# Delta rule of a hybrid decoder layer: the inverse applied to the residual inside the chain, fill products tied to the chain's links, and zero-block buffers made once

## The chip, the cores and the metric

The kernel runs on one core of one Trainium2 chip. The metric is the device time of one execution in microseconds (us); lower is better. The core has a matrix engine (TensorE; PE in the profile, with its weight loads as PEld), a vector engine (DVE), a scalar engine (ScalarE; ACT), a general engine (GpSimd; POOL) and a queue for loads and stores (SyncE; SP). Each engine works through its own list of instructions and waits for the others by semaphores.

## What is computed

One decoder layer: an RMS norm, one input projection, then two mixers side by side (a gated delta rule over 4 heads of 128, and dilated attention over 8 heads of 64), gates, and one output projection with the residual. The sequence has 2048 tokens. The part that matters here is the delta rule, in chunks of 64 tokens:

```python
l_mat = a_mat + jnp.eye(CHUNK)                       # a_mat strictly lower
u = triangular_solve(l_mat, vc * bc[..., None])
w = triangular_solve(l_mat, kb * jnp.exp(gc)[..., None])
...
def step(state, inp):
    a_i, qd_i, kt_i, u_i, w_i, gl_i = inp
    v_new = u_i - jnp.einsum('bhck,bhkv->bhcv', w_i, state)
    o_i = jnp.einsum('bhck,bhkv->bhcv', qd_i, state) + jnp.einsum('bhij,bhjv->bhiv', a_i, v_new)
    state = state * gl_i[..., None, None] + jnp.einsum('bhck,bhcv->bhkv', kt_i, v_new)
    return state, o_i
```

Since `u` and `w` are the same inverse applied to two right sides, `v_new` is also that inverse applied to the difference `beta v - exp(g) beta k state`. The state goes from chunk to chunk, 32 steps in a row for each head.

## The kernel before

The kernel projects the sequence (`conv_proj`, `gate_proj`: `pj` products of 128x512), prepares the inverses of the triangular matrices (`stage1a`, `inverse`), runs the delta rule, and then attention and the output projection. Projections and output use pairs of high and low parts, three products for one.

The delta rule handles heads in two pairs; a pair's two heads lie side by side in the 128 partitions, 64 tokens each. Four chunks make a group.

- `stage2` (L614, 16 calls: 8 groups by 2 pairs) prepares a group of one pair. It loads `kT`, `qT`, `vT`, the rows `Qr`, the mask `E`, the inverse's blocks `TT` and `D0`; completes the inverse with 32x32 products (L650, L657); forms `at` (L665, L674), the squares of q (L662, in a buffer `tmp`) and their sums (L668); turns k and v (L688); scales them to `Kc` (L691), `Ks` (L694) and `kV` (L698). Then `pw = Kc TT` (L701), copied into `WQ` (L704), and `pu = TT kV` (L707), copied to `U` (L709), each four products. The other half of `WQ` is q times `Qr` (L634, GpSimd). Buffers with blocks of zeros (`at_`, `Ks`) are set to zero by GpSimd in every call (L670, L671, L681, L682); `TT` has two buffers that are zeroed once.
- `chain` (L720, 64 calls) is one chunk of one pair: two `C` products of the state with `WQ` (L727), two vector additions to `VN` (L731), two `SU` products (L733), two vector operations to the new state `S` (L737), the product with `at` (L741), its copy (L742), two additions to the output `o4` (L745) and its squares (L747). `SU` is one tile for both pairs; `C` has two buffers.
- `dn_out` (L749) scales a group's output (`zs`, L762) and stores it.
- `proj_fill` (L908) is the attention's input projection: 2304 `pj` products of 128x256 in 12 sets of 192, with the splitting of its weights (`wh` on ScalarE, `wl` on the vector engine, 1024 columns) and the work behind a finished tile (`t`, `ss`, `qs`, products `pm`). These products are the fills: they have the lowest priority, and the first 960 (`HOLD * 192`, L963) may go before the chain's end.

The order on each engine is set when the program is built: a scheduler takes, at each point, the ready instruction with the lowest priority number, where `chain` starts at 1000000, `dn_out` too, `stage2` at 1200000, the second gate projection at 1900000 and the fills at 2400000. `add_manual_dep(..., NOSYNC)` ties an instruction behind another in the order of the same engine, without a semaphore. A buffer that is written again waits for its readers.

I call both pairs' work on one chunk a link.

Of the kernel before, what the change touches and what calls it, by code (L numbers as in the profile page):

```python
# [16 lines left out]
P = 128  # L17
# [20 lines left out]
HOLD = 5  # L38
PATT0 = 2400000
# [45 lines left out]
def hybrid(tc, xT, x, norm_w, w_in, conv_w, a_log, dt_bias, dn_norm_w, q_norm_w, k_norm_w,  # L85
# [521 lines left out]
    TTz = [dn.tile([P, 4, P], F32, name=f"TTz{i}") for i in range(2)]  # L607
    for t in TTz:
        nc.gpsimd.memset(t[:CH, :, CH:], 0.0)
        nc.gpsimd.memset(t[CH:, :, :CH], 0.0)  # L610
    turn2 = [0]
    SU = psD.tile([P, 4, P], F32, name="SU", bufs=1)

    def stage2(pair, c0, dma2=dma):  # L614
# [18 lines left out]
        for s_ in range(2):  # L633
            nc.gpsimd.tensor_tensor(WQ[:, :, s_, (1 - s_) * CH:(2 - s_) * CH], Qr[:, :, s_], qT[:, :, 1 - s_],  # L634
                                    op=ALU.mult)
# [25 lines left out]
        q2 = dn.tile([P, 4, P], F32, name="tmp", bufs=2)  # L661
# [7 lines left out]
        at_ = dn.tile([P, 4, P], F32, name="at_", bufs=3)  # L669
        nc.gpsimd.memset(at_[:CH, :, :CH], 0.0)  # L670
        nc.gpsimd.memset(at_[CH:, :, CH:], 0.0)  # L671
# [8 lines left out]
        Ks = dn.tile([P, 4, 2, P], F32, name="Ks", bufs=3)  # L680
        nc.gpsimd.memset(Ks[:CH, :, 1], 0.0)  # L681
        nc.gpsimd.memset(Ks[CH:, :, 0], 0.0)  # L682
        Kc = dn.tile([P, 4, P], F32, name="tmp", bufs=2)
        kV = dn.tile([P, 4, P], F32, name="tmp", bufs=2)
        for w, src in enumerate((kT, vT)):
            tp = psD.tile([P, 4, P], F32, name="A", bufs=2)
            for u in range(4):
                nc.tensor.transpose(tp[:, u], src[:, u].rearrange("p s i -> p (s i)"), ident)  # L688
            if w == 0:
                for u in range(4):  # L690
                    nc.scalar.mul(Kc[:, u], tp[:, u], negc_u[:, u0 + u:u0 + u + 1])  # L691
                for s_ in range(2):
                    a = slice(s_ * CH, (s_ + 1) * CH)
                    nc.vector.tensor_tensor(Ks[a, :, s_], tp[a], sk[a, 0, :, None].to_broadcast([CH, 4, P]),  # L694
                                            op=ALU.mult)
# [3 lines left out]
        pw = psD.tile([P, 4, P], F32, name="A", bufs=2)  # L699
        for u in range(4):  # L700
            nc.tensor.matmul(pw[:, u], Kc[:, u], TT[:, u], start=True, stop=True)  # L701
        for s_ in range(2):
            a = slice(s_ * CH, (s_ + 1) * CH)
            nc.vector.tensor_copy(WQ[:, :, s_, a], pw[:, :, a])  # L704
        pu = psD.tile([P, 4, P], F32, name="A", bufs=2)
        for u in range(4):
            nc.tensor.matmul(pu[:, u], TT[:, u], kV[:, u], start=True, stop=True)  # L707
# [3 lines left out]
        return dict(WQ=WQ, at=at_, Ks=Ks, U=U, o4=o4, D0=d0)  # L711
# [3 lines left out]
    for pair in range(2):  # L715
        s0 = dn.tile([P, 2, P], F32, name=f"S{pair}", bufs=2)
        nc.vector.memset(s0, 0.0)
        Sst.append(s0)

    def chain(pair, c, g):  # L720
# [4 lines left out]
        pc, po, su = pcs[:, 0:2], pcs[:, 2], SU[:, 2 * pair:2 * pair + 2]  # L725
        for s_ in range(2):
            nc.tensor.matmul(pc[:, s_], g["WQ"][:, u, s_], S0[:, s_], start=True, stop=True)  # L727
        VN = dn.tile([P, P], F32, name="VN", bufs=4)
        for s_ in range(2):
            a = slice(s_ * CH, (s_ + 1) * CH)  # L730
            nc.vector.tensor_tensor(VN[a], pc[a, s_], g["U"][a, u], op=ALU.add)  # L731
        for s_ in range(2):
            nc.tensor.matmul(su[:, s_], g["Ks"][:, u, s_], VN, start=True, stop=True)  # L733
        S1 = dn.tile([P, 2, P], F32, name=f"S{pair}", bufs=2)
        for s_ in range(2):
            h = 2 * pair + s_
            m = nc.vector.scalar_tensor_tensor(S1[:, s_], S0[:, s_], egl[c % 2][:, h * NT + c // 2:h * NT + c // 2 + 1],  # L737
                                           su[:, s_], op0=ALU.mult, op1=ALU.add)
        Sst[pair] = S1
        mark[c] = m  # L740
        mark["pe"] = nc.tensor.matmul(po, g["at"][:, u], VN, start=True, stop=True)  # L741
        nc.scalar.copy(g["o4"][:, u], po)  # L742
        for s_ in range(2):
            b = slice((1 - s_) * CH, (2 - s_) * CH)
            nc.vector.tensor_tensor(g["o4"][b, u], pc[b, s_], g["o4"][b, u], op=ALU.add)  # L745
# [162 lines left out]
    def proj_fill():  # L908
# [4 lines left out]
        n = 0  # L913
        for s_ in range(12):
# [3 lines left out]
            for o8 in range(8):  # L918
# [30 lines left out]
                for kt in range(KT):  # L949
# [5 lines left out]
                    for x_, w_ in ((xh, 0), (xh, 1), (xl, 0)):  # L955
                        while posts and posts[0][0] <= n:
                            posts.pop(0)[1]()
                        if s_ < 11 and o8 == 7 and kt == 2 and w_ == 0 and x_ is xh:
# [3 lines left out]
                                             stop=kt == KT - 1 and x_ is xl)  # L962
                        if n == HOLD * 192:  # L963
# [600 lines left out]
```

## Time and profile before

| what | us |
|---|---|
| median of 3 runs (lowest, highest) | 1385.46 (1384.54, 1389.88) |
| the profiled execution | 1385.32 |
| its span | 1383.5 |
| TensorE busy in 480 to 780 us by `pj` products of 128x256 (three groups of rows) | 96.1, 95.0, 94.8 |
| TensorE busy, 750 to 800 us, of 50 | 45.54 |
| TensorE busy, 800 to 900 us, of 100 | 96.62 |

How to read it: a row of a group names the line, the engine, the operation and the tiles (out <- in), then a count, busy time and mean; behind it stands the idle time of the engine just ahead of those instructions, and what ended it. A row of the timeline has its start, its length, and in brackets the idle time ahead of it. A product of float32 has two records, and `x4` of L733 is two products. Matmuls overlap, so the distance between the starts, not the length, is what one costs TensorE; the chain of waits shows that distance. Clock is the granted share of TensorE's full clock.

### The profile page before, as it was taken

How to read it: one execution, taken by the hardware profiler on the slowest of the kernel's cores; microseconds unless marked ns; L12 is line 12 of the kernel's file. 1: busy time of each engine (PE TensorE's matmuls, PEld its weight loads, DVE VectorE, ACT ScalarE, POOL GpSimd, SP SyncE). 2: the span in 40 equal slices, each digit the busy share in tenths (PEclk: the TensorE clock that was granted, in tenths of full speed). 3: DMA queues.
4: the chain of work that ended last, by engine and by line, in shares of the span. 5: the costliest groups of instructions: out<-in, count | busy, mean ns of one | idle time of the engine just before them, and what ended most of it. 6: DMA issues, size and time to landing. Idle time of an engine off the chain costs nothing.

```text
span 1383.5 us, 28812 instructions
## 1 busy us (share of the span) xinstructions
PE 1360.6 (98%) x10262; PEld 1215.8 (88%) x10262; DVE 857.3 (62%) x2724; ACT 675.8 (49%) x1930; POOL 484.7 (35%) x572
## 2 busy tenths in 40 slices
PE   8999999999999999999999999999999999999998
PEld 7998787778888789999999889999998888888877
DVE  7534668899652358787787565635454746555565
ACT  5644525573322234444444476566666655555520
POOL 3000000000761204442342423574857384655500
PEclk9999999999999999999999999999999999999999
DMA  6654526756647846657553455264647786655764
GB/s 191 185 105 90 110 57 146 162 128 116 110 84 143 205 108 155 156 147 195 132 149 78 108 138 134 78 185 97 177 116 240 200 253 162 198 163 175 207 196 144
DMA packets 301324, 205.01 MB, mean 148 GB/s; under 512 B 149324, under 2 KB 271068, under 8 KB 300669
## 3 DMA queue, kind: packets, MB, share of 16 engines
q1 hardware_dynamic: 230652, 171.09, 49.3%
q10 hardware_dynamic: 70528, 32.09, 8.5%
q8 instruction: 81, 1.33, 0.4%
q14 instruction: 63, 0.51, 0.1%
HBM read 142.61 MB, written 60.50 MB: 147 GB/s over the span
## 4 chain that ended last, share of the span: by engine, by line
PE 85%; DVE 6%; DMA 4%; ACT 3%; issue 2%; ACTq 0%; SPq 0%; POOL 0%; DVEq 0%
PE pj L99 18%; PE po L99 10%; PE sc L99 8%; PE pj L208 7%; PE pj L207 7%; PE pj L206 7%; PE pz L99 6%; PE pv L99 5%; PE pt L99 4%; PE SU L733 2%; PE C L727 2%; PE pm L99 1%; PE A L665 1%; PE A L688 1%; PE A L701 1%
## 5 line engine op out<-in xcount | busy, mean ns | idle before, releaser
L99 PE MATMUL pj<-wh,xh 128*128 128x256 f32 (+1 forms) x776 | 226.9, 292 | 1.3 <-DVE ml L99 1.3
L99 ACT ACTIVATE pr<-pr,ml 128x192 f32<-128x192 f32 (+2 forms) x384 | 156.8, 409 | 146.1 <-DVE ml L99 132.3
L99 PE MATMUL pj<-wh,xl 128*128 128x256 f32 (+1 forms) x776 | 224.6, 289 | 0.0
L99 PE MATMUL pj<-wl,xh 128*128 128x256 f32 (+1 forms) x776 | 224.3, 289 | 0.0
L208 PE MATMUL pj<-xh,wl 128*128 128x512 f32 x512 | 203.5, 397 | 0.7 <-DVE wl L192 0.7
L206 PE MATMUL pj<-xh,wh 128*128 128x512 f32 x512 | 202.6, 396 | 0.0
L207 PE MATMUL pj<-xl,wh 128*128 128x512 f32 x512 | 202.6, 396 | 0.0
L99 PE MATMUL po<-xh,mh 128*128 128x512 f32 x424 | 147.9, 412 | 1.0 <-ACT mh L99 0.7
L99 PEld LDWEIGHTS pj<-wh,xh 128*128 128x128 f32 x776 | 146.4, 189 | 2.5 <-issue 2.2
L99 PEld LDWEIGHTS pj<-wh,xl 128*128 128x128 f32 x776 | 146.5, 189 | 0.5 <-issue 0.3
L99 PEld LDWEIGHTS pj<-wl,xh 128*128 128x128 f32 x776 | 146.6, 189 | 0.1
L99 DVE CUSTOM_DVE_ANT_0 pr<-sc,bias 128x192 f32<-128x192 f32 (+2 forms) x384 | 100.0, 307 | 68.6 <-PE sc L99 67.7
L478 DVE SCALAR_TENSOR_TENSOR cy<-cu,cw,cy 128x512 f32<-128x512 f32 x144 | 111.6, 775 | 19.3 <-ACT cy L476 17.1
L208 PEld LDWEIGHTS pj<-xh,wl 128*128 128x128 f32 x512 | 96.2, 188 | 23.3 <-DVE wl L192 1.1
L207 PEld LDWEIGHTS pj<-xl,wh 128*128 128x128 f32 x512 | 96.2, 188 | 22.2
L206 PEld LDWEIGHTS pj<-xh,wh 128*128 128x128 f32 x512 | 96.3, 188 | 21.7
L99 POOL COPY qz<-q 64x512 f32<-64x512 f32 x96 | 95.0, 989 | 51.7 <-PE sc L99 38.8
L99 DVE COPY pT<-pt 64x128 f32<-64x128 f32 (+2 forms) x220 | 69.4, 323 | 64.7 <-PE pt L99 61.3
L543 POOL MEMSET inv<- 128x1024 f32 x1 | 1.0, 954 | 259.5 <-DVE cu L474 259.5
L99 POOL TENSOR_TENSOR Fb<-Fb,op 128x256 f32<-128x256 f32 x84 | 71.5, 865 | 57.6 <-DMA Fb<-F 29.7
L99 PEld LDWEIGHTS po<-xh,mh 128*128 128x128 f32 x424 | 77.9, 189 | 14.2 <-DVE mh L99 1.2
L99 PE MATMUL po<-xl,mh 128*128 128x512 f32 x212 | 86.5, 408 | 0.0
(371 smaller groups left out, 3068.5 us busy)
## 6 DMA issues: line engine op xcount, KB each, us to landing
wraw<-in_w_in SPq DMA_DIRECT2D x44, 512.0 KB, 7.1
cv<-cy ACTq DMA_DIRECT2D x48, 256.0 KB, 2.6
Fb<-F SPq DMA_DIRECT2D x64, 192.0 KB, 5.2
xr<-in_xT SPq DMA_DIRECT2D x32, 256.0 KB, 4.0
kT<-cv SPq DMA_DIRECT2D x32, 256.0 KB, 3.3
qk<-qs ACTq DMA_DIRECT2D x64, 128.0 KB, 4.2
res<-in_x SPq DMA_DIRECT2D x13, 512.0 KB, 4.9
V<-v_d SPq DMA_DIRECT2D x20, 256.0 KB, 4.9
```

The lines of the kernel that those rows point to most:

```text
L99: i = f(*args, **kw)
L206: nc.tensor.matmul(ps, wh[:, k, c * P:(c + 1) * P], xh[tb][:, kt, :], start=kt == 0, stop=False)
L207: nc.tensor.matmul(ps, wh[:, k, c * P:(c + 1) * P], xl[tb][:, kt, :], start=False, stop=False)
L208: nc.tensor.matmul(ps, wl[:, k, c * P:(c + 1) * P], xh[tb][:, kt, :], start=False, stop=kt == KT - 1)
L478: nc.vector.scalar_tensor_tensor(y, u[:, i:i + 512], cw[:, ct, i:i + 1], y, op0=ALU.mult, op1=ALU.add)
L543: eng.memset(Tt, 0.0)
L665: nc.tensor.matmul(pq[:, u], kT[:, u].rearrange("p s i -> p (s i)"), qT[:, u].rearrange("p s i -> p (s i)"), start=True, stop=True)
L688: nc.tensor.transpose(tp[:, u], src[:, u].rearrange("p s i -> p (s i)"), ident)
L701: nc.tensor.matmul(pw[:, u], Kc[:, u], TT[:, u], start=True, stop=True)
L727: nc.tensor.matmul(pc[:, s_], g["WQ"][:, u, s_], S0[:, s_], start=True, stop=True)
L733: nc.tensor.matmul(su[:, s_], g["Ks"][:, u, s_], VN, start=True, stop=True)
```

## The change

1. **The inverse in the chain.** `stage2` no longer makes `Kc`, `pw`, `pu` and `U`. The half of `WQ` that held `pw` now holds k itself, copied by GpSimd. In `chain` the two `C` products give k (and q) times the state; the vector engine forms the residual `R = kV - exp(g) C`; one more product (`TT`, L727 of the new program) applies the inverse; ScalarE copies the result to `VN`. Chunk 0 has no state, so it skips the `C` products and the additions to the output; chunk 31 skips the `SU` products and the new state.
2. **Fills held to the links.** For the links of chunks 1 to 30, a dictionary `gates` ties fills 0, 15, 23 (then 32 more for each link) behind the last `WQ`, `TT` and `SU` product of that chunk: 15, 8 and 9 fills a link, 960 in all.
3. **Zero blocks in lists.** `TT` has four buffers, `at` and `Ks` three; their zeros are written once, at the start. The squares of q go to the buffer of `Qr`; `kV` has a buffer of its own.
4. **Pair 1's preparation** is written behind the group's four links, no longer behind the first.

```diff
+LINK0 = 1
+FILL = (15, 8, 9)
...
+    TTs = zeroed("TT", 4, [P, 4, P], True)
+    ATs = zeroed("at", 3, [P, 4, P], False)
+    KSs = zeroed("Ks", 3, [P, 4, 2, P], "half")
...
+            nc.gpsimd.tensor_copy(WQ[:, :, s_, s_ * CH:(s_ + 1) * CH], kT[:, :, s_])
...
-        TT = TTz[n2 % 2]
+        TT = TTs[n2 % 4]
...
-        q2 = dn.tile([P, 4, P], F32, name="tmp", bufs=2)
+        q2 = Qr.rearrange("p u s i -> p u (s i)")
...
-                for u in range(4):
-                    nc.scalar.mul(Kc[:, u], tp[:, u], negc_u[:, u0 + u:u0 + u + 1])
...
-        for u in range(4):
-            nc.tensor.matmul(pw[:, u], Kc[:, u], TT[:, u], start=True, stop=True)
...
-            nc.vector.tensor_copy(WQ[:, :, s_, a], pw[:, :, a])
...
-            nc.tensor.matmul(pu[:, u], TT[:, u], kV[:, u], start=True, stop=True)
-        U = dn.tile([P, 4, P], F32, name="U", bufs=3)
-        nc.scalar.copy(U, pu)
...
+        R = g["kV"][:, u]
+        if c:
+            for s_ in range(2):
+                mark[c, 0] = nc.tensor.matmul(pc[:, s_], g["WQ"][:, u, s_], S0[:, s_], start=True, stop=True)
+            R = dn.tile([P, P], F32, name="R", bufs=2)
+            for s_ in range(2):
+                a = slice(s_ * CH, (s_ + 1) * CH)
+                nc.vector.scalar_tensor_tensor(R[a], pc[a, s_], negc_u[a, col:col + 1], g["kV"][a, u],
+                                               op0=ALU.mult, op1=ALU.add)
+        mark[c, 1] = nc.tensor.matmul(pn, g["TT"][:, u], R, start=True, stop=True)
+        VN = dn.tile([P, P], F32, name="VN", bufs=3)
+        nc.scalar.copy(VN, pn)
+        S1 = None
+        if c < 31:
+            for s_ in range(2):
+                mark[c, 2] = nc.tensor.matmul(su[:, s_], g["Ks"][:, u, s_], VN, start=True, stop=True)
...
-            if u == 0:
-                for p_ in range(2):
-                    if c0 + 4 < 32:
-                        G[p_] = at_prio("prep", stage2, p_, c0 + 4)
+            if u == 0 and c0 + 4 < 32:
+                G[0] = at_prio("prep", stage2, 0, c0 + 4)
+        if c0 + 4 < 32:
+            G[1] = at_prio("prep", stage2, 1, c0 + 4)
...
+        gates, k = {}, 0
+        for c in range(LINK0, 31):
+            for part in range(3):
+                gates[k] = (c, part)
+                k += FILL[part]
...
+                        if n in gates:
+                            tc.add_manual_dep(m.ins, mark[gates[n]].ins.name, NOSYNC, reason="no sooner than this link")
```

How this moves instructions, at three places. The numbers in the names tell buffers apart: `S_...` is a state, `at_...`, `Ks_...` and `TT_...` a pair's buffer of a group; `pj` rows are fills.

First, TensorE inside a link. Before, near the middle of the stage, this stands between the `SU` products of the two pairs; nine more fills follow the last row, and then the other pair's `SU`:

```order
L733 MATMUL SU<-VN,Ks 128x128 x2
L741 MATMUL C<-VN,at__5609 128x128
L657 MATMUL A<-TTz_4473,Xs 32x32 x6
L741 MATMUL C<-VN,at__5507 128x128
L657 MATMUL A<-TTz_4473,Xs 32x32 x2
L665 MATMUL A<-qT,kT 128x128 x4
L99 MATMUL pj<-wh,xl_139 128x256
```

In the change, the link of chunk 30 has this, and so have eight other links:

```order
L733 MATMUL SU<-VN,Ks_4496 128x128 x2
L744 MATMUL C<-VN,at_4487 128x128
L744 MATMUL C<-VN,at_4485 128x128
L733 MATMUL SU<-VN,Ks_4494 128x128 x2
L101 MATMUL pj<-wh,xh_140 128x256
L101 MATMUL pj<-wl,xh_140 128x256
```

The fills that stood between the pairs now stand behind the second `SU`.

Second, TensorE at the chain's end. Before, these rows are the last links, with the next fill four rows after the last one shown:

```order
L727 MATMUL C<-S_7294,WQ 128x128 x2
L733 MATMUL SU<-VN,Ks 128x128 x2
L741 MATMUL C<-VN,at__7074 128x128
L741 MATMUL C<-VN,at__6972 128x128
L733 MATMUL SU<-VN,Ks 128x128 x2
L727 MATMUL C<-S_7311,WQ 128x128 x2
L727 MATMUL C<-S_7328,WQ 128x128 x2
L733 MATMUL SU<-VN,Ks 128x128 x2
L741 MATMUL C<-VN,at__7074 128x128
L741 MATMUL C<-VN,at__6972 128x128
L733 MATMUL SU<-VN,Ks 128x128 x2
```

In the change, chunk 31 alone stands between fills:

```order
L101 MATMUL pj<-wh,xl_141 128x256
L721 MATMUL C<-S_7131,WQ 128x128 x2
L721 MATMUL C<-S_7151,WQ 128x128 x2
L727 MATMUL C<-R,TT_4475 128x128
L744 MATMUL C<-VN,at_4487 128x128
L727 MATMUL C<-R,TT_4476 128x128
L744 MATMUL C<-VN,at_4485 128x128
L101 MATMUL pj<-wh,xh_138 128x256
```

The fills that were used up earlier now last to the end of chunk 30.

Third, the vector engine where a group begins (one of the middle groups before, chunk 12 in the change). Before, one pair's outputs `zs` (L762) stand here, and the other pair's come a link later:

```order
L737 SCALAR_TENSOR_TENSOR S_5735<-S_5701,egl_120,SU 128x128 x2
L731 TENSOR_TENSOR VN<-C,U 64x128 x2
L759 SCALAR_TENSOR_TENSOR f<-ssqo,f 128x4
L675 COPY ssqq<-A 128x4
L694 TENSOR_TENSOR Ks<-A,sk 64x4x128 x2
L762 SCALAR_TENSOR_TENSOR zs<-o_5189,f,zs 128x128 x4
L731 TENSOR_TENSOR VN<-C,U 64x128 x2
L737 SCALAR_TENSOR_TENSOR S_5752<-S_5718,egl_120,SU 128x128 x2
L745 TENSOR_TENSOR o_5291<-C,o_5291 64x128 x2
```

In the change, behind the residual of pair 1 (the row ahead of the first one shown is a small one):

```order
L765 SCALAR_TENSOR_TENSOR zs<-o_5103,f,zs 128x128 x4
L684 TENSOR_TENSOR at_4487<-A,E_5726 64x4x64 x2
L761 TENSOR_SCALAR f<-ssqq 128x4
L765 SCALAR_TENSOR_TENSOR zs<-o_5301,f,zs 128x128 x4
L738 SCALAR_TENSOR_TENSOR S_5683<-S_5538,egl_119,SU 128x128 x2
L761 TENSOR_SCALAR f<-ssqq 128x4
L101 TENSOR_TENSOR wl<-wraw,wh 128x4x256
L748 TENSOR_TENSOR o_5446<-C,o_5446 64x128 x2
L748 TENSOR_TENSOR o_5644<-C,o_5644 64x128 x2
L699 TENSOR_TENSOR Ks_4496<-A,sk 64x4x128 x2
L685 COPY ssqq<-A 128x4
L738 SCALAR_TENSOR_TENSOR S_5703<-S_5558,egl_119,SU 128x128 x2
```

Both pairs' outputs, a weight split and the new `Ks` now stand between the residual of pair 1 and its new state.

More of the change, by code (lines that the diff above doesn't have):

```diff
@@ L679, in stage2 @@
         nc.gpsimd.tensor_tensor(sk[:, 1], sk[:, 1], phalf[:, :4], op=ALU.pow)
[L680 to L684, printed above, removed]
+        Ks = KSs[n2 % 3]
+        kV = dn.tile([P, 4, P], F32, name="kV", bufs=3)
         for w, src in enumerate((kT, vT)):
@@ L715, in hybrid @@
     for pair in range(2):
-        s0 = dn.tile([P, 2, P], F32, name=f"S{pair}", bufs=2)
-        nc.vector.memset(s0, 0.0)
-        Sst.append(s0)
+        Sst.append(None)
     def chain(pair, c, g):
@@ L724, in chain @@
         pcs = psD.tile([P, 4, P], F32, name="C", bufs=2)
[L725 to L738, printed above, removed]
+        pc, po, pn, su = pcs[:, 0:2], pcs[:, 2], pcs[:, 3], SU[:, 2 * pair:2 * pair + 2]
+        R = g["kV"][:, u]
[7 more added lines that the diff above has]
+                                               op0=ALU.mult, op1=ALU.add)
```

36 lines of the change are left out of this document (20 added, 16 removed).

## The prediction

> **What bounds the kernel now.** I read the page first, then busy time by stretch, then the chain of waits inside the stage that the change touches. That stage is the delta rule, whose `SU` products run from 484 to 777 us.
>
> ```profile
> L733 PE MATMUL SU<-VN,Ks x256: 270/275/377, 484.3 to 777.2; 128*128 128x128 f32 x128
> ```
> ```profile
> span 1383.5 us, 28812 instructions
> PE 1360.6 (98%) x10262; PEld 1215.8 (88%) x10262; DVE 857.3 (62%) x2724; ACT 675.8 (49%) x1930; POOL 484.7 (35%) x572
> ```
>
> The span is 1383.5 us; the profiled execution took 1385.3, so 1.8 lies around the span. The median of the runs shown is 1385.46, which is the same within 0.2 us, and I sum against 1385.3. The busy shares are an average, so the stage comes next (columns: stretch, length, busy us of PE, PEld, DVE, ACT, POOL, granted clock, DMA share, GB/s).
>
> ```profile
> 560.00:570.00 10.00, 10.00 (x101) 9.84 (x101) 8.87 (x28) 4.22 (x18) 6.32 (x12) 1.00 0.60 159
> 760.00:770.00 10.00, 8.72 (x70) 8.02 (x68) 6.90 (x19) 3.77 (x10) 2.81 (x4) 1.00 0.52 109
> 770.00:780.00 10.00, 7.85 (x56) 6.77 (x56) 8.54 (x31) 3.31 (x13) 1.86 (x2) 1.00 0.39 37
> ```
>
> TensorE is full in the middle of the stage and has holes only at its end. The vector engine stands close behind it, 8.87 of 10 us where a group of four chunks begins. The chain of waits (500 to 760 us, then pieces of 560 to 580) says the same: nearly all of it is TensorE.
>
> ```profile
> by line: PE pj L99 42.9%; PE C L727 10.1%; PE SU L733 9.7%; PE A L665 5.5%; PE A L688 5.2%; PE C L741 5.2%; PE A L701 4.8%; PE A L707 4.8%; PE A L668 4.2%; PE pm L99 2.2%; PE A L657 2.2%; PE A L650 2.2%; PE pm L596 0.6%; DVE ss L99 0.3%; DV
> ```
> ```profile
> 560.43 0.37 PE A L657 x16
> ...
> 563.36 0.44 PE SU L733 x4
> ...
> 564.25 0.79 PE A L668 x8
> ...
> 568.43 0.44 PE A L688 x4
> ...
> 572.42 0.89 PE A L707 x8
> 573.31 1.07 PE pj L99 x9
> ...
> 576.60 1.09 PE A L665 x8
> ```
>
> From these I take TensorE's prices. One float32 product of 128x128 is two records: 0.89 / 4 = 0.2225 us. One fill product is 1.07 / 9 = 0.119 us. So an instruction less on TensorE is time less, as long as something is always ready for it. Whether it is, is the question here.
>
> **What the change removes from TensorE.** Each of the 16 preparations loses `pw` (L701) and `pu` (L707), 8 products: 128 in all. Each of the 64 steps of the chain (32 chunks, 2 pairs) gains one, the inverse on the residual: 64. Chunk 0 loses its four products with the zero state, chunk 31 its four updates of a state that nobody reads: 8. Net 128 - 64 + 8 = 72 products, 72 x 0.2225 = **-16.0 us**. The 960 fill products ahead of the chain's end stay 960.
>
> **The end of the stage.** Today the fills run out three chunks early, and the last links stand bare:
>
> ```profile
> 765.48 0.61 PE L733 MATMUL SU<-VN,Ks 128*128 128x128 f32 x4
> ...
> 767.04 0.60 DVE L737 SCALAR_TENSOR_TENSOR S<-S,egl,SU 128x128 f32<-128x128 f32 x2
> ...
> 767.53 0.68 PE L727 MATMUL C<-S,WQ 128*128 128x128 f32 x4 [0.88 <-DVE S L737]
> ...
> 773.79 0.61 DVE L737 SCALAR_TENSOR_TENSOR S<-S,egl,SU 128x128 f32<-128x128 f32 x2 [0.18 <-PE SU L733]
> ```
> ```profile
> 774.45 0.71 PE L733 MATMUL SU<-VN,Ks 128*128 128x128 f32 x4 [0.25 <-DVE S L737]
> ...
> 776.81 0.71 PE L733 MATMUL SU<-VN,Ks 128*128 128x128 f32 x4 [0.96 <-DVE VN L731]
> ...
> 777.50 0.36 PE L99 MATMUL pj<-wh,xh 128*128 128x256 f32 x1
> ```
>
> From 765.48 to 777.50 are 12.0 us; in them the order has 27 products (6.0 us) and one fill, so 5.9 us are lost. With the fills dealt out by link only chunk 31 is bare. It has two hops (residual, then the copy of `VN`), and one such hop costs 0.96 in the row above: 1.9 us. Gain **-4.0 us**.
>
> **What the change adds: waits inside each link.** Now a low-priority fill goes wherever TensorE would be idle. After the change 15, 8 and 9 fills are tied behind the `WQ`, `TT` and `SU` products of a link, so no fill can stand elsewhere. What the vector engine needs is shown by its rows:
>
> ```profile
> 559.63 0.69 DVE L99 TENSOR_TENSOR t<-pj,ss 128x512 f32<-128x512 f32 x1
> ...
> 561.48 0.86 DVE L674 TENSOR_TENSOR at__5242<-A,E 64x256 f32<-64x256 f32 x2
> ...
> 563.84 0.61 DVE L737 SCALAR_TENSOR_TENSOR S<-S,egl,SU 128x128 f32<-128x128 f32 x2 [0.30 <-PE SU L733]
> ...
> 564.98 1.14 DVE L762 SCALAR_TENSOR_TENSOR zs<-o,f,zs 128x128 f32<-128x128 f32 x4
> ...
> 566.75 1.39 DVE L694 TENSOR_TENSOR Ks<-A,sk 64x512 f32<-64x512 f32 x2
> 568.17 0.59 DVE L731 TENSOR_TENSOR VN<-C,U 64x128 f32<-64x128 f32 x2
> ```
> ```profile
> 765.90 1.23 DVE L99 TENSOR_TENSOR wl<-wraw,wh 128x1024 fp32r<-128x1024 f32 x1 [1.48 <-ACT wh L99]
> ```
> ```profile
> 774.43 1.21 DVE L745 TENSOR_TENSOR o<-C,o 64x128 f32<-64x128 f32 x4
> ```
>
> *Bare link.* Pair 1's `SU` waits for pair 0's state update, since both lie in one tile: today at 774.45, 0.05 after the update's end. The update starts 0.48 after `SU` is issued (563.36 to 563.84) and lasts 0.61, so `SU` of pair 1 goes 1.14 after that of pair 0. TensorE has 0.44 and the two `at` products, 0.89, to do meanwhile. Wait 0.25. Nine links have nothing else there: 2.3 us.
>
> *Weight split.* In five links the vector queue has `wl` between the two pairs' updates, in two of them `t` as well. Pair 1's update then starts at 0.48 + 0.61 + 1.23 + 1.21 = 3.53, its second half is there at 4.19, and the last `WQ` product ends 0.22 later, at 4.41. TensorE alone would be there at 1.14 + 0.44 + 1.07 + 0.89 = 3.54. Wait 0.87, with `t` 1.56: 3 x 0.87 + 2 x 1.56 = 5.7 us. Behind a waiting `WQ` the whole queue of TensorE stands, fills too.
>
> *Group starts.* Both pairs' output products `zs` now fall into one link; today they are a link apart. In the worst group (rows in the section on the change) pair 1's update comes after two `zs` (2.28), `at` 0.86, `S` 0.61, `wl` 1.23, `o` 1.21, `Ks` 1.39 and some 0.3 of small ones: 7.9 us behind its residual, and `WQ` 0.49 later (767.04 to 767.53), 8.4. TensorE needs `TT` 0.22, eight fills 0.95, `SU` 0.44, `at` 0.45, `kT` 0.44, L668 0.79, `SU` 0.44, nine fills 1.07, `WQ` 0.45, `vT` 0.44, 0.37: 6.1, after a lag of about 1 us (15 fills 1.8 and L665 1.09 against `t`, a copy and two residuals, about 2): 7.1. Wait 1.3. In the link before, `at`, `Ks` and `o` ahead of pair 1's update cost 0.9 in the same way: 2.2. In the best group `Ks` is behind both updates, and some 0.6 is left. Seven groups at 1.4: 9.8 us; between the ends I take the middle, as the orders of the other groups lie between these two.
>
> Sum of the waits 2.3 + 5.7 + 9.8 = **+17.8 us**. Its ends: 2.3, if only the bare links wait; about 33, if each of 30 links waits 0.25 + 0.87.
>
> **What costs nothing, and its cover.**
>
> ```profile
> L691 ACT ACTIVATE tmp<-A,negc_u 128x128 f32<-128x128 f32 x60 | 17.1, 368 | 16.3 <-PE A L688 16.1
> ...
> L742 ACT COPY o<-C 128x128 f32<-128x128 f32 x64 | 16.7, 265 | 61.1 <-PE C L741 60.8
> ```
>
> ScalarE loses the 64 scalings of L691 (17 us) and the 16 copies `U`, and gains 64 copies of `VN` like L742 (17 us); at 4.2 busy of 10 it has room. A copy stands in the chain, 0.27 behind `TT`, under eight fills (0.95). Without that cover: 0.3 to 0.6 a link, 9 to 18 us. The vector engine loses the 32 copies of L704. GpSimd loses 64 memsets and gains 16 more at the start and 32 copies like L634 below, 0.73 each; it is busy 6.3 of 10 at its fullest above. At the start they stand ahead of the first `WQ`, which waits for `Qr` anyway: 0, at worst 3 us.
>
> Pair 1's preparation is written behind the four links, and its loads with it. On SP one `Qr` stands behind `y_d` and `zs`, and it waits for the products of L668, since the squares lie in its buffer.
>
> ```profile
> L631 SPq DMA_DIRECT2D Qr<-rows_d x32: 359/495/2879, 447.2 to 716.6; - x32
> ...
> DMA to landing us min/median/max: 3.6/4.6/6.7
> ```
> ```profile
> L643 SPq DMA_DIRECT2D TTz<-A x28: 573/588/2583, 476.1 to 721.7; - x28
> ...
> DMA to landing us min/median/max: 2.2/4.2/9.0
> ```
> ```profile
> L634 POOL TENSOR_TENSOR WQ<-Qr,qT x32: 721/731/1160, 456.1 to 742.0; 128x256 f32<-128x256 f32 x32
> ```
> ```profile
> L762 DVE SCALAR_TENSOR_TENSOR zs<-o,f,zs x64: 335/346/819, 526.3 to 782.5; 128x128 f32<-128x128 f32 x64
> ```
>
> Two issues of 0.5, 4.6 to land, three GpSimd operations of 0.73 and a square of about 0.6 make 8.4 us; TensorE asks for the squares a link and a half later, 9 to 10. The inverse's buffer is free only after a group's last link and is read about 6 us later; 1.2 + 4.2 = 5.4. Both fit at the median: 0. At the longest landings they miss by 1 and 4 us, up to 5 a group.
>
> **Sum.** 1385.3 - 16.0 - 4.0 + 17.8 = 1383.1; I say **1383 us**. Outside the stage nothing is added, and the attention behind it begins as soon as the chain ends.
>
> **Rivals.** *The fills cover the hops as they do today.* For it: in 500 to 760 us hardly a wait of TensorE is left, with the same vector work. Against it: those fills were free to go anywhere. Waits of 2.3 alone give 1385.3 - 20.0 + 2.3 = 1368 us (1364 to 1374).
>
> *The vector engine and late loads set the link's pace: slower.* Its work in the first link of a group (the 7.9 above, four half residuals, `t` and a copy, about 10.4 us) is more than TensorE's (6.1, then `WQ`, 15 fills and the rest, about 9), and a late `TT` or `Qr` stops TensorE's queue at the same place. It decides from a mean wait of 0.7 us a link: then 20 is lost. At 30 us it gives 1395 (1390 to 1402).
> On this the Trainium skill has a rule (SBUF — State Buffer, section Who interferes with whom): a vector instruction with two inputs in SBUF contends with a GpSimd instruction that reads SBUF, not with one that only writes. The change puts reading copies in place of writing memsets. The longest `zs`, 819 ns against 346, may be such a meeting, and the longest L634, 1160 against 731, too. By the rule the 14 groups of `zs` of the stage would lose up to 0.47 each, 6.6 us, and the time would be 1388. It has a small chance of its own, as both rows' medians lie at their shortest.
>
> *It doesn't do what it says:* the scheduler leaves fills out of place, or the removed products cost less than 0.2225 because they hid in other waits. Then some 1387.
>
> **How the numbers follow.** Forecast (waits take back most, 1372 to 1393) 0.5; cover holds 0.22; vector engine and loads 0.20; the meeting of vector engine and GpSimd 0.03; the last 0.05. A change below 0.5% (6.9 us) can't be told from none here, so "faster" is under 1378.4 and "slower" over 1392.2. Faster: 0.22 and a third of the forecast's case, 0.38. Slower: 0.20 and the last bit of the forecast's case, 0.22. Same: the rest, 0.40. The range reaches from the middle of the first rival to the middle of the second, with the waits' ends: 1366 to 1397.
>
> **What would show it.** Right: L701 and L707 gone, `SU` to `SU` in bare links 1.1 us apart, TensorE waits named `WQ` after `S` at five `wl` links and at group starts, the bare end shorter by 4 us, the time between first and last `SU` shorter by some 1 to 4 us. Wrong: TensorE busy throughout with no such waits (first rival), or waits at L668 and L650 for loads and 20 or more us of waits for the vector engine (second).

## The result and the profile after

| | before | after |
|---|---|---|
| median, us (lowest to highest) | 1387.05 (1384.54 to 1389.88), 4 runs | 1403.44 (1398.62 to 1408.89), 4 runs |
| ratio, with its 95% interval | | 1.0119 (1.01 to 1.0139) |
| the profiled execution, us | 1385.3 | 1408.89 |

The change makes the kernel 16 us slower; 1383 was forecast, 1366 to 1397 the range. The profiled execution of after is the slowest of its four, 5.4 us over the median. From the page and from the row of `SU`:

```profile
span 1407.0 us, 28403 instructions
PE 1363.5 (97%) x10118; PEld 1210.1 (86%) x10118; DVE 845.9 (60%) x2676; ACT 666.4 (47%) x1914; POOL 475.1 (34%) x556
```
```profile
L733 PE MATMUL SU<-VN,Ks x248: 270/275/583, 481.0 to 790.8; 128*128 128x128 f32 x124
```

TensorE has 144 records less, which are the 72 products, and is drawn busy 3 us longer. The stage's place is seen from the first fill behind the chain:

```profile
796.47 0.36 PE L101 MATMUL pj<-wh,xh 128*128 128x256 f32 x1
```

Before, that row stood at 777.50: the chain ends 19.0 us later. From there to the end of the span are 610.5 us, against 606.0 before. So 23.5 = 19.0 in the stage + 4.5 behind it.

**The work itself.** What TensorE's own work comes to can be estimated from starts: every record gets the mean distance to the next start that records of its shape have in before from 500 to 740 us (0.131 us for a fill, 0.108 for half a float32 product of 128x128). From 440 us to the chain's end this adds up to 331.9 us in before and 317.0 in after, 14.9 less. Priced by pairs of neighbouring shapes instead, it is 13.5 less. So the forecast's -16.0 came nearly whole, and the time was lost again elsewhere.

**Holes in the stage.** What TensorE waited for, 481 to 797 us (total, times, longest):

```profile
PE SU L733 <- DVE S L738: 4.3, 12, 1.1
PE C L721 <- DVE o L748: 4.0, 7, 0.9
PE SU L733 <- ACT VN L729: 2.9, 2, 2.5
PE A L695 <- issue: 2.4, 2, 1.2
PE A L662 <- PE C L721: 1.2, 2, 0.6
...
PE C L721 <- DVE S L738: 0.6, 3, 0.2
```

The whole list comes to 18.0 us in 35 holes. Before, from 484 to 778 us, it is some 3.3 in 6, all at the bare end:

```profile
PE SU L733 <- DVE VN L731: 1.6, 2, 1.0
PE C L727 <- DVE S L737: 1.1, 2, 0.9
PE C L741 <- DVE VN L731: 0.4, 1, 0.4
PE SU L733 <- DVE S L737: 0.3, 1, 0.3
```

And the list understates. In a bare link (one with nothing else for TensorE to do), on the timeline of after (start, length),

```profile
677.34 0.61 PE L733 MATMUL SU<-VN,Ks 128*128 128x128 f32 x4
677.78 0.61 PE L744 MATMUL C<-VN,at 128*128 128x128 f32 x4
678.65 0.71 PE L733 MATMUL SU<-VN,Ks 128*128 128x128 f32 x4 [0.25 <-DVE S L738]
```

four records cost 0.44 (677.34 to 677.78), so TensorE was free from 678.22, and the next product went at 678.65: 0.43 lost, 0.25 listed, because the last product's record is drawn 0.18 beyond the point at which the next could start. If the 29 further holes are like this one, that is some 5 us on top of 14.7, an estimate.

**The clock.** The longest hole on the timeline, with what ScalarE, GpSimd and the vector engine did, and busy time in the stretches after it (the granted clock is third from the end):

```profile
654.78 1.22 PE L733 MATMUL SU<-VN,Ks 128*128 128x128 f32 x4 [2.51 <-ACT VN L729]
```
```profile
653.95 0.63 ACT L674 ACTIVATE Qr<-qT 128x512 f32<-128x512 f32 x1 [3.36 <-POOL WQ L645]
654.48 0.41 ACT L729 COPY VN<-C 128x128 f32<-128x128 f32 x2
```
```profile
652.13 1.78 POOL L645 TENSOR_TENSOR WQ<-Qr,qT 128x256 f32<-128x256 f32 x1 [1.08 <-DMA Qr<-rows_d]
```
```profile
652.12 1.21 DVE L101 TENSOR_TENSOR wl<-wraw,wh 128x1024 fp32r<-128x1024 f32 x1
```
```profile
650.00:655.00 5.00, 2.49 (x21) 2.29 (x21) 4.85 (x15) 1.53 (x4) 3.48 (x3) 0.96 0.93 286
655.00:660.00 5.00, 5.00 (x37) 4.71 (x38) 3.16 (x9) 1.87 (x8) 0.00 (x0) 0.50 0.40 114
660.00:665.00 5.00, 5.00 (x37) 4.65 (x37) 1.47 (x5) 0.30 (x2) 0.00 (x0) 0.52 0.44 133
```

Read it backwards. `SU` waits for the copy of `VN`; that copy stands on ScalarE behind the squares of q, which are written into `Qr` and so wait for GpSimd to have read it, and GpSimd waits for the load of `Qr`; its product then takes 1.78 us (0.73 is usual) beside the vector engine's `wl`. The hole is 2.5 us, and behind it TensorE runs at half clock for 10 us: 37 records in each 5 us, and 58 in the 5 us that follow, so 4.9 us more are lost. In these stretches TensorE reads as fully busy. Two other places of the stage (455 to 460 at 0.66, 535 to 545 at 0.85 and 0.81) lose 3.4 in the same way. The Trainium skill (TensorE: Matmul & The Clock Gate, Part 1: The HAM clock gate) has half clock come after an idle window of about 3.4 us; here a hole of 2.5 was enough.

The chain ends 19.0 us later with 14.9 us less work, so 34 us are to be found: 14.7 of listed holes, 5 of unlisted, 8.3 of clock. Some 6 are left in steps too short for any list; where they lie isn't shown. The experiments turn to these.

**Behind the stage.** The timeline of after, then that of before: the first splits of the attention on the vector engine, and ScalarE's table load ahead of the first exponential.

```profile
814.60 2.99 DVE L101 SCALAR_TENSOR_TENSOR xl<-big,nw,xh 128x512 fp32r<-128x512 f32 x2 [3.95 <-ACT xh L101]
817.51 2.92 DVE L101 TENSOR_TENSOR wl<-wraw,wh 128x1024 fp32r<-128x1024 f32 x1
...
809.67 1.28 ACT L101 ACT_TABLE_LOAD   x1 [4.78 <-DMA qk<-qs]
810.97 0.35 ACT L101 ACTIVATE pr<-pr,ml 128x64 f32<-128x64 f32 x1
...
821.80 2.89 PE L101 MATMUL sc<-K,qz 128*128 128x192 f32 x8 [3.84 <-DVE ml L101]
```
```profile
794.40 1.42 DVE L99 SCALAR_TENSOR_TENSOR xl<-big,nw,xh 128x512 fp32r<-128x512 f32 x2 [2.74 <-ACT xh L99]
795.96 1.92 DVE L99 TENSOR_TENSOR wl<-wraw,wh 128x1024 fp32r<-128x1024 f32 x1
...
786.85 1.28 ACT L99 ACT_TABLE_LOAD   x1 [0.94 <-ACT qs L99]
790.64 0.35 ACT L99 ACTIVATE pr<-pr,ml 128x64 f32<-128x64 f32 x1 [2.51 <-DVE ml L99]
```

Before, the load was done 2.5 us ahead of the exponential. After, it comes only behind the wait for `ml`: the row names a transfer, but the vector engine's first `ml` ended at 809.59, and the load starts at 809.67. Everything behind it on ScalarE is 1.3 us later, and the splits (0.75 for each `xl` and 1.22 for `wl` at their medians) then lie for most of their length beside two long copies of GpSimd (814.40 to 819.35) and take about twice as long. TensorE waits 3.84, and its clock falls to 0.68 for 5 us.

### The profile page after: what moved, and what is told of

Its sections match the earlier page's. It is cut to its first block, busy times and chain, and to the rows that moved or that the text cites. A ratio compares the mean times of both kernels' runs of the same rounds, so it can differ in the third digit from the quotient of the medians.

```text
span 1407.0 us, 28403 instructions
## 1 busy us (share of the span) xinstructions
PE 1363.5 (97%) x10118; PEld 1210.1 (86%) x10118; DVE 845.9 (60%) x2676; ACT 666.4 (47%) x1914; POOL 475.1 (34%) x556
## 4 chain that ended last, share of the span: by engine, by line
PE 78%; DVE 8%; DMA 7%; issue 2%; ACT 2%; SPq 1%; POOL 0%; ACTq 0%; DVEq 0%; POOLq 0%
PE pj L101 15%; PE po L101 10%; PE sc L101 7%; PE pj L210 7%; PE pj L209 7%; PE pj L208 7%; PE pz L101 6%; PE pv L101 5%; PE pt L101 4%; PE SU L733 2%; PE C L721 2%; DMA V<-v_d 1%; PE pm L101 1%; DMA Qr<-rows_d 1%; PE C L727 1%
## 5 line engine op out<-in xcount | busy, mean ns | idle before, releaser
L480 DVE SCALAR_TENSOR_TENSOR cy<-cu,cw,cy 128x512 f32<-128x512 f32 x144 | 111.5, 775 | 19.5 <-ACT cy L478 17.5
L210 PEld LDWEIGHTS pj<-xh,wl 128*128 128x128 f32 x512 | 96.3, 188 | 23.5 <-DVE wl L194 1.0
L101 PEld LDWEIGHTS po<-xh,mh 128*128 128x128 f32 x424 | 77.9, 189 | 14.2 <-DVE mh L101 1.2
```

The lines of the kernel that those rows point to most:

```text
L101: i = f(*args, **kw)
L210: nc.tensor.matmul(ps, wl[:, k, c * P:(c + 1) * P], xh[tb][:, kt, :], start=False, stop=kt == KT - 1)
L480: nc.vector.scalar_tensor_tensor(y, u[:, i:i + 512], cw[:, ct, i:i + 1], y, op0=ALU.mult, op1=ALU.add)
```

## The experiments

Cover is the other work that TensorE has while a link waits for another engine. Theories: **A**, the ties hold fills out of the holes; **B**, the squares' buffer puts a load in front of the `VN` copies; **C**, pair 1's preparation is too late; **D**, a link with two more hops needs more cover than there is, and the removed products were cover; **E**, a hop hides under free fills. Later **F** (the shared `SU` tile), **G** (the shares 15, 8, 9), **H** (the table load). Medians are compared with before on the same chip.

### Ties away, squares apart, preparation back, ties alone

```diff
-                        if n in gates:
-                            tc.add_manual_dep(m.ins, mark[gates[n]].ins.name, NOSYNC, reason="no sooner than this link")
```

> The kernel after, with the fills free again (the line that ties every 15th, 8th and 9th fill to a product of a link is gone); all else as after. Theory A (the ties keep fills out of the holes): the holes of TensorE in the stage, 18 us as listed, mostly close, the clock stays at 1.00, and the time falls to 1375 to 1388 us. Theory B (the squares in the buffer of Qr make ScalarE wait for a load, with the VN copies of two links behind it): the long hole before SU and the clock loss behind it stay, time 1395 to 1403. Theory C (both pairs' outputs, Ks and o in one link): within 5 us of after. If the free fills run out early, the last links stand bare and the time is above 1403.

Measured 1410.89 (before 1387.12; 1.017, 1.0155 to 1.0185): 7 us worse than after. A in this form falls, and the busy time of the stage says why:

```profile
500.00:600.00 100.00, 100.00 (x952) 96.80 (x951) 65.19 (x184) 39.46 (x119) 32.46 (x41) 1.00 0.54 146
600.00:700.00 100.00, 100.00 (x949) 97.37 (x949) 65.19 (x183) 39.38 (x122) 29.52 (x38) 1.00 0.60 153
700.00:800.00 100.00, 81.76 (x625) 69.59 (x625) 78.04 (x254) 37.45 (x151) 24.50 (x35) 0.91 0.38 90
```

With free fills TensorE has no hole for 200 us, though the vector engine has the same work as after: that engine doesn't set the pace while there is cover. Then the fills are used up: the last one goes at 703.54 us, and in the last 100 us 18 are lost in holes and 9 in clock.

```diff
-        q2 = Qr.rearrange("p u s i -> p u (s i)")
+        kV = dn.tile([P, 4, P], F32, name="kV", bufs=3)
+        q2 = kV
```

> The kernel after, but the squares of q go into the buffer that kV takes later, so that neither they nor the next load of Qr wait for each other. Theory B: ScalarE's 22 us of waiting before L674 in 9 places go, no SU waits 2.5 us for VN, no stretch of the stage has a granted clock of 0.5, and the time falls by 7 to 10 us, to 1393 to 1397. Theory A and theory C: the square was a single accident, time 1400 to 1404.

Measured 1397.92 (1.0077, 1.0062 to 1.0092), 5.5 us under after. The hole for `VN` at 652 us is gone, and with it the 10 us at half clock (5 us at 0.66 are left in the stage). B holds, a little under the expected size.

```diff
-        if c0 + 4 < 32:
-            G[1] = at_prio("prep", stage2, 1, c0 + 4)
+            if u == 0 and c0 + 4 < 32: G[1] = at_prio("prep", stage2, 1, c0 + 4)
```

> The kernel after, with the second pair's preparation written behind the first link of a group again, as before the change. Theory C (pair 1's loads and preparation come too late and fall into one link with the outputs): the waits for o (L748) and for S by group starts halve, Qr and D0 are loaded a link or more sooner, time 1393 to 1398. Theory A: no change beyond 3 us, 1400 to 1406. Theory B: no change or worse, as the two preparations share the one Qr buffer: 1403 to 1410.

Measured 1401.82 (1.0113, 1.0091 to 1.0135), but this can't be read: with lists of three, `at` and `Ks` of the next group are written over pair 0's while three of its links still need them, so those links compute with other data and wait for other writers. It was done again with turning buffers:

```diff
-        at_ = ATs[n2 % 3]
+        at_ = dn.tile([P, 4, P], F32, name="at_", bufs=3)
+        nc.gpsimd.memset(at_[:CH, :, :CH], 0.0)
...
-        Ks = KSs[n2 % 3]
+        Ks = dn.tile([P, 4, 2, P], F32, name="Ks", bufs=3)
```

> The kernel after, with the second pair's preparation written behind the first link of a group again, and at and Ks in turning buffers with their memsets again, as the list of three can't be written that early. Theory C (late loads and all vector work of a group start in one link): 1392 to 1398, the waits of WQ for o (L748 of after) and of L662 at most half. Otherwise 1400 to 1408.

Measured 1402.78 (1.0119, 1.0102 to 1.0136), as after: neither the place of the preparation nor the memsets matter. C falls.

```diff
+            mark[c, 0] = nc.tensor.matmul(pc[:, s_], g["WQ"][:, u, s_], S0[:, s_], start=True, stop=True)
...
+FILL = (16, 16)
```

> The kernel before, with nothing changed but ties: 16 fills behind the WQ products and 16 behind the SU products of each link from chunk 1 to 30. Theory A (ties cost the waits): slower than before by 8 to 20 us, 1395 to 1407, less some 4 us for the last links that are no longer bare. Theories B and C: the same as before or up to 6 us faster, 1381 to 1388, with the last links no longer bare.

Measured 1393.08 (1.0041, 1.0026 to 1.0056). The ties cost before 6 us, although its last links are no longer bare. That is inside A's 8 to 20 less 4, and B and C expected no cost. Its trace is 8.1 us longer than that of before: 3.5 up to the chain's end (780.99 us) and 4.6 behind it.

### What a product and a hop are worth

```diff
-        for u in range(4):
-            nc.tensor.matmul(pw[:, u], Kc[:, u], TT[:, u], start=True, stop=True)
+        nc.tensor.matmul(pw[:, 0], Kc[:, 0], TT[:, 0], start=True, stop=True)
...
+            nc.vector.tensor_copy(WQ[:, :, s_, a], pw[:, 0, None, a].to_broadcast([P, 4, CH]))
```

> The kernel before, with three of the four products of pw and of pu left out in every preparation (96 in all) and their first result copied four times, so that the other engines do what they did; the output is therefore another. If a product is worth its time on TensorE (the first term of the prediction): 96 x 0.2225 = 21.4 us less, 1366 us. If the products were cover under which the links waited (theory D): the fills run out sooner, the last links stand bare longer, and half or less is gained, 1376 to 1387.

Measured 1373.60 (before 1385.93; 0.9908, 0.9893 to 0.9923): 12.3 us less for 96 products, 0.13 each of 0.2225, between the two expectations. On TensorE the products were worth their time: by the estimate above, its work up to the chain's end falls by 20.6 us of 21.4. But the last fill goes at 737.13 us, and up to the chain's end at 765.82 the links stand bare, 28.7 us in place of 11.2 in before (766.29 to 777.50). The stage loses 9 us more than in before, 5.2 of them to the clock in this stretch:

```profile
740.00:760.00 20.00, 17.45 (x106) 14.86 (x106) 17.95 (x63) 7.81 (x32) 5.54 (x9) 0.74 0.48 78
```

```diff
+        V0 = dn.tile([P, P], F32, name="V0", bufs=1)
...
+        VN = dn.tile([P, P], F32, name="VN", bufs=3)
+        nc.scalar.copy(VN, V0)
```

> The kernel before, with one more hop in each link: VN goes through a copy on ScalarE ahead of SU (64 copies), fills free. Theory D (a longer link needs more cover than there is): the fills run out sooner and the time rises by 8 us or more, over 1395. Theory E (a hop hides under free fills; the cost of the change is in its ties, buffers and places): within 3 us of before, 1384 to 1390.

Measured 1396.47 (1.0068, 1.0052 to 1.0084): +10.5 us for copies on an engine that is busy less than half the time, without one product or tie changed. E falls, and D's size holds. The fills don't run out sooner, as D expected (the last goes at 765.66 us), but from there to the chain's end are 19.5 us, in the fastest of the four executions (1392.25). The new `V0` has one buffer for both pairs; the vector engine's listed waits for the copy, 0.9 us in 3 places, are too small to be the cause.

```diff
+        nc.tensor.matmul(pcs[:, 3], ident, V0, start=True, stop=True)
+        VN = dn.tile([P, P], F32, name="VN", bufs=3)
+        nc.scalar.copy(VN, pcs[:, 3])
```

> The kernel before, with two more hops in each link, as after has them: VN goes through a product with the identity and a copy on ScalarE ahead of SU (64 products, 64 copies); preparations, fills and buffers as before. The copy alone gave +10.5 (e6_one_more_hop). If the sum of the parts is the cause (theory D): the product adds its 14.2 us on TensorE (64 x 0.2225) and some 4 at the first attention link, where ScalarE here waits for GpSimd ahead of its table load as in after: 1409 to 1416. If the product hides like the fills it stands among: 1395 to 1402.

Measured 1423.59 (before 1387.42; 1.0272, 1.0253 to 1.029): +36.2, more than D's sum. The product and its hop cost 25.6 on top of the copy. Its time on TensorE is 14.3 of that by the same estimate (14.2 expected), and the trace has 4.4 more behind the chain; the rest are further waits. The last fill goes at 729.55 us, 81.4 us ahead of the chain's end:

```profile
740.00:760.00 20.00, 17.93 (x161) 15.78 (x160) 16.86 (x57) 10.29 (x40) 5.84 (x10) 1.00 0.52 148
760.00:780.00 20.00, 16.86 (x186) 15.50 (x185) 16.13 (x56) 9.27 (x36) 4.31 (x7) 1.00 0.32 87
780.00:800.00 20.00, 14.94 (x103) 12.23 (x100) 16.10 (x57) 8.13 (x34) 5.04 (x8) 1.00 0.19 41
```

### Where the fills stand, and the shared tile

```diff
-            for part in range(3):
-                gates[k] = (c, part)
-                k += FILL[part]
+            gates[k] = (c, 0)
+            k += sum(FILL)
```

> The kernel e2_squares_own, with one tie a link in place of three: 32 fills no sooner than the WQ products of their link, free inside it. Theory A in its second form (not the share per link but the fixed 15, 8 and 9 leave the holes): the waits of WQ for o and S and of SU for S shrink, 1383 to 1391. Theory D (a link has less cover than hops, wherever it stands): the holes only move inside the link, 1395 to 1402. If all 32 go behind the first hop, above 1402.

Measured 1406.62 (1.0143, 1.0113 to 1.0173), 9 us above e2_squares_own, as expected for fills that all go early: in a bare link all 32 now stand ahead of the first `SU`, 20 of them behind pair 0's `WQ` products. Free inside the link, they stand where the scheduler puts them, not where the chip has its holes; `WQ` waits for `o` up to 2.4 us, the clock is 0.988.

```diff
-        pc, po, pn, su = pcs[:, 0:2], pcs[:, 2], pcs[:, 3], SU[:, 2 * pair:2 * pair + 2]
+        pc, po, pn, su = pcs[:, 0:2], SU[:, pair], pcs[:, 2], pcs[:, 2:4]
```

> The kernel e2_squares_own, with the state products of each pair in that pair's own tile (behind C, where the inverse's result was read out), and the output products of both pairs in the tile SU; so SU of pair 1 no longer waits for pair 0's state update. Theory F (the shared tile makes a hole in each bare link, 13 listed waits of 0.25 and some 0.16 more each that overlap with the product before): the waits of SU for S go and the time falls by 3 to 6 us, to 1392 to 1395. Theory D (a link has too little cover): the hole moves to the next WQ, within 2 us of 1398.

```diff
-FILL = (15, 8, 9)
+FILL = (12, 8, 12)
```

> The kernel e2_squares_own, with 12, 8 and 12 fills behind WQ, TT and SU in place of 15, 8 and 9. Theory G (the 32 fills of a link are enough, but three too many stand where the residual is long done and three too few ahead of the next WQ): the waits of WQ for o and S, 5 us listed, go, 1390 to 1394. Theory D: the residual's hop opens in their place, 1396 to 1400.

Measured 1397.90 (1.0074, 1.0054 to 1.0094) and 1397.68 (1.0072, 1.0059 to 1.0086): neither edit gains anything. The waits show what D said: the first has no `SU` after `S` any more, but the next hops open; in the second `WQ` waits less for `o` (1.4 in place of 3.0), and `SU` more (5.4 in place of 3.3).

```profile
PE C L721 <- DVE o L748: 7.0, 10, 1.5
...
PE C L727 <- DVE R L725: 3.0, 4, 1.1
PE C L733 <- ACT VN L729: 2.9, 5, 1.6
```
```profile
PE SU L733 <- DVE S L738: 5.4, 14, 0.7
...
PE C L721 <- DVE o L748: 1.4, 4, 0.5
```

> Both edits of e9_su_by_pair and e10_other_shares on e2_squares_own. If both gains hold and add (F and G): 1384 to 1390. If only one of them holds: 1391 to 1395. Theory D: 1395 to 1399.

Measured 1390.55 (before 1387.01; 1.0028, 1.0014 to 1.0042). Together they gain 7.4 us. Which hole closes isn't plain: the listed wait of `WQ` for `o` is 7.1, as with the tile alone, and that of the `SU` products for `VN` 1.3 in place of 2.9. Here D's expectation fails; part of the lost cover is a matter of place.

```diff
+        gates = {960 - 32 * (31 - c): c for c in range(KEEP, 31)}
```

> The kernel before, with chunk 0's products with the zero state and chunk 31's state products left out as in after, and the last 96 fills kept for links 28 to 30 (32 no sooner than each one's WQ); preparations, hops and buffers as before. The prediction's terms for this are -1.8 (8 products) and -4.0 (the bare end), together 1381. If the bare end costs the same wherever the fills stand (theory D): 1384 to 1387.

Measured 1390.92 (1.0024, 1.0013 to 1.0035): 4 us slower than before, not 6 faster, and above both expectations. In its trace the attention's start costs 4.6 us, as in after (598.4 us from the first `sc` product to the end, against 593.8). The stage gains nothing either: the chain ends at 778.83 us, 1.3 later than in before, where 5.8 less was forecast. Kept for the last links, the fills are missing elsewhere, and `WQ` waits 1.46 for `o` at 658 us.

### The table load

The program tells why the load comes later. In after, the output of the first exponential lies where `WQ` lay, which GpSimd was the last to write, so the exponential waits for two engines, and one of the two waits, that for the vector engine, stands as an instruction of its own ahead of the load. In before that output lies where `at` lay, and the exponential waits for the vector engine alone. A new writer isn't needed for this: in e12_before_kept the output lies where `Ks` lay, in e13_two_hops where `at` lay, both with zeros from GpSimd as in before, and there too the exponential waits for both and the load is late. A short copy that reads `WQ` earlier takes that wait out:

```diff
+        if c == 30 and pair:
+            nc.scalar.copy(dn.tile([P, P], F32, name="jk", bufs=1)[:, :1], g["WQ"][:, 3, 1, P - 1:P])
```

> The kernel after, with one short copy on ScalarE in chunk 30 that reads WQ, so that ScalarE has waited for GpSimd's last write of WQ before the first exponential of the attention, whose output lies where WQ lay. Theory H (in after that exponential has two waits, one of them therefore stands ahead of the table load, and the load's 1.28 us make the splits behind it meet GpSimd's copies): the table load starts before the wait, the 3.8 us wait for ml falls to about 1, the time from the first attention product to the end goes from 598 to 594, the median to 1398 to 1400. Otherwise 1401 to 1405.

Measured 1400.30 (1.0101, 1.0083 to 1.0119), 3 us under after; as the two intervals overlap, the size rests on the trace, where the time from the first `sc` product to the end falls from 598.3 to 595.3 (594 was expected). The load is back ahead of the wait and the splits at their old length:

```profile
801.98 1.28 ACT L101 ACT_TABLE_LOAD   x1 [1.42 <-issue]
805.28 0.35 ACT L101 ACTIVATE pr<-pr,ml 128x64 f32<-128x64 f32 x1 [2.02 <-DVE ml L101]
...
808.99 1.41 DVE L101 SCALAR_TENSOR_TENSOR xl<-big,nw,xh 128x512 fp32r<-128x512 f32 x2 [2.68 <-ACT xh L101]
810.55 1.94 DVE L101 TENSOR_TENSOR wl<-wraw,wh 128x1024 fp32r<-128x1024 f32 x1
```

TensorE's longest wait for `ml` falls from 3.8 to 1.1. So H holds for the load and the splits; the median lies just above its range. This run shows one thing more. At 650 us it has the same order as after, but the second half of `Qr` came about 1 us sooner and met no `wl`; the hole for `VN` was 0.48, and the clock stayed:

```profile
652.15 0.71 PE L735 MATMUL SU<-VN,Ks 128*128 128x128 f32 x4 [0.48 <-ACT VN L729]
```
```profile
650.00:655.00 5.00, 3.59 (x42) 3.11 (x41) 4.88 (x14) 1.98 (x7) 3.03 (x3) 1.00 0.90 264
655.00:660.00 5.00, 5.00 (x57) 4.78 (x56) 4.76 (x15) 1.95 (x8) 0.00 (x0) 1.00 0.46 127
```

So one landing can make several us. The spread of the executions goes with the clock: of the six of this run the one of 1407.65 has a mean clock of 0.991, the others, 1398.97 to 1401.49, have 0.995 to 0.997. In after, 1408.89 and 1406.40 have 0.992 and 0.994, 1398.62 and 1400.48 have 0.995 and 0.996.

> The kernel e11_both with the short copy of e14_pool_wait_early. By theory H 3 to 5 us less than e11_both: 1385 to 1388, level with before. If the wait was covered there: 1389 to 1392.

Measured 1388.42 (before 1387.42; 1.0016, 1.0003 to 1.0029): between the two expectations. The squares' own buffer, the divided tile with 12, 8 and 12 fills, and the short copy bring the change level with before, not under it.

```diff
-FILL = (12, 8, 12)
+FILL = (12, 7, 13)
```

> The kernel e15_all_three, with 12, 7 and 13 fills in place of 12, 8 and 12. If the next WQ is still what waits most (7 us listed for o): 1 to 3 us less than e15_all_three. If the hops are now in balance (theory D): the same or up to 3 us more, as the copy of VN has less cover.

Measured 1391.33 (1.0032, 1.002 to 1.0043), 3 us more: `TT` after `R` waits 6.2 in place of 2.8. No run was under before, but for e5_fewer_products, which leaves work out.

## Why the prediction was wrong

**The step that failed** is the sum of what takes the removed work back: "Sum of the waits 2.3 + 5.7 + 9.8 = **+17.8 us**", with -4.0 for the end, nothing for the clock, and "Outside the stage nothing is added". The -16.0 itself held as work. For the profiled execution of after, against before:

| part | forecast | in the traces |
|---|---|---|
| work on TensorE | -16.0 | -14.9 |
| holes and short steps, the bare end with them | +17.8 - 4.0 | +25.6 |
| clock in the stage | 0 | +8.3 |
| behind the stage | 0 | +4.5 |
| sum, us | -2.2 | +23.5 |

This execution is 5.4 us over the median, and its mean clock is the lowest of the four, so the median has less of the clock's share.

Behind the failed step stands a condition that the prediction wrote down itself: "an instruction less on TensorE is time less, as long as something is always ready for it". It didn't hold. Only 960 fills cover 64 steps of the chain, and what the preparation computes is cover as well. The change takes that work away and makes each step longer. With free fills (e1_no_ties) the stock is used up 90.6 us ahead of the chain's end, in before 11.2; dealt out by link, 32 to each, the fills leave the holes listed above. The prediction looked for holes at three kinds of place and priced each by its own length.

Tried alone, the parts of the change cost this, with holes and clock in every row:

| part | from | us |
|---|---|---|
| 128 products of the preparation removed | -12.3 / 96 each | -16.4 |
| a product and a copy more in each link (with the late table load) | e13_two_hops | +36.2 |
| 8 products of chunks 0 and 31 removed | the forecast's price, not measured alone | -1.8 |
| fills tied 15, 8, 9 | after less e1_no_ties, 16.4 - 23.8 | -7.4 |
| squares in `Qr` | after less e2_squares_own, 16.4 - 10.8 | +5.6 |
| sum | | +16.2 |
| measured | 1403.44 - 1387.05 | +16.4 |

These are net prices, so none can be set beside one term of the forecast. Each part was measured in other surroundings than the rest, the first is scaled up from 96 products, and of the -7.4 for the ties 4.3 lie behind the chain in the traces (614.8 us from the first fill behind the chain to the end in e1_no_ties, 610.5 in after). The close fit is luck. What holds is the order of size: two hops more cost over 30 us, far more than the work that was saved.

- *Waits, +17.8.* Right in kind, too small, and at other places: `WQ` waited for `o`, a reader of its `C` buffer, far more than for `S` at the weight splits (4.0 against 0.6); the bare link's hole is 0.43, not 0.25.
- *The clock, costed at nothing.* The miss of up to 5 us a group for late loads was written down, but not what a hole does to the clock: 4.9 us behind the one at 652 us.
- *The end, -4.0.* The last links of after are indeed better covered, but e12_before_kept shows no gain in the stage.
- *ScalarE "has room".* True and beside the point: it works through its list in order, and the squares in front of the `VN` copies passed a late load on to `SU` (5.6).
- *"Outside the stage nothing is added."* Wrong by 3 to 4.6: an exponential that waits for one engine more, because of what lay in its memory half a stage before.
- *The rivals.* "Vector engine and late loads" named 1395 and the loads; the vector engine isn't the bound while there is cover (e1_no_ties). "The cover holds" is refuted by the same run's last 100 us. The meeting of vector engine and GpSimd did occur, not at `zs` but in the attention's splits; its price was summed wrongly too, as 1383.1 + 6.6 is 1389.7, not 1388. The last rival, removed products that cost less than their time, came nearest to the cause, with a chance of 0.05 and 1387.

What stays open is where the some 6 us in short steps lie, and how much of the lost cover is place: e11_both got back 7.4 us by moving fills and a tile.

## What to carry to other kernels

Where a latency chain is covered by a fixed stock of other work, work that you remove from the busy engine is partly cover: the work saved is real, but ask when the stock runs out, and price each new hop by what it takes from the stock, not by its own 0.27 us (10.5 us for 64 copies here). Before you put a copy into the chain, look at what stands ahead of it on its engine's queue, and what that waits for. And read a change of buffer or writer through to the next use of the same memory.

## What the runs showed of the hardware

- Behind a hole of 2.5 us TensorE ran at half clock for 10 us; behind three of together 1.4 in the same place it didn't. The length of one hole doesn't decide it: at 455 us the wait for `D0t` was 1.6 in e16_shares_again, with a clock of 0.80 and 0.86 in the next two stretches of 5 us, and 2.0 in e5_fewer_products with 1.00 in both. In after it was 1.8, with 0.66 behind it, in before 1.6 with 1.00. What decides it no run here shows.
- The split `wl` took 2.92 us beside GpSimd's copies, 1.22 at its median; GpSimd's L645 took 1.78 beside `wl`, 0.73 at its median. The Trainium skill (SBUF — State Buffer, Who interferes with whom) says that a vector instruction with two SBUF inputs contends with a GpSimd instruction that reads SBUF; the trace agrees, and here the price was at places where the forecast didn't look.
